# Hybrid network kernel: a third attention traced earlier, and a new order of projection chunks and output k-tiles

## The chip, the core and the metric

One core of a Trainium2 chip runs the whole kernel. The metric is the device time of one execution in microseconds; times given for a kernel are medians over its runs. Five engines work in order, each through its own queue of instructions: TensorE (PE in the profile, with its weight loads as PEld), VectorE (DVE), ScalarE (ACT), GpSimd (POOL) and SyncE (SP, which here issues the transfers from memory).

## The reference

The network has two blocks. The first is two "hybrid layers" on 256 tokens of width 1024; the second is one mixer (a state-space scan and an attention) and a mixture of 16 experts. The change is in the hybrid layer:

```python
def hybrid_layer(x, norm_w, w_in, w_out, conv_w, pe_cmp, w_cmp_k, w_cmp_v, pool_w, pool_scale):
    h = rmsnorm(x, norm_w)
    p = split_cols(h @ w_in)
    o_a = dsa_mixer(...)
    o_b = nsa_mixer(...)
    o_c = shortconv_mixer(p['c_b'], p['c_c'], p['c_x'], conv_w)
    o_d = pool_mixer(p['d_u'], pool_w, pool_scale)
    mixed = jnp.concatenate([jax.nn.silu(p['a_gate']) * o_a, jax.nn.silu(p['b_gate']) * o_b,
                             jax.nn.silu(p['c_gate']) * o_c, jax.nn.silu(p['d_gate']) * o_d], axis=-1)
    return x + mixed @ w_out
```

`dsa_mixer` is an attention over the keys that an index score picks; `nsa_mixer` is gated compressed attention plus two causal ones; `shortconv_mixer` is `b * conv(c * x)` with three taps; `pool_mixer` is a running mean over 2 to 16 tokens, less the token, times a small matrix. Each branch is 256 wide.

## The kernel before, in words

All arithmetic is in float32. A matrix product with full accuracy is made of three: each operand is split into a high and a low part, and `mm3` (L419, L420, L421) adds high by high, high by low and low by high. The weights are split on the chip piece by piece, the high part `whi` by ACT (L318), the low part `wlo` by DVE (L319).

The weights come as a stream of chunks of up to 2 MB in the order of the table `CHUNKS`, into a ring of four buffers; SP issues each transfer, and a buffer is given back as soon as its last piece is split. `run_pieces` takes the chunks piece by piece: it traces the split of the next piece at high priority, then runs the matmuls of the piece before, then that piece's closing work (`post_...`), and then grants the *side queue* a fixed credit (`SIDE_RATE`, 2.0 in layer 0 and 2.4 in layer 1). The side queue (`Side`) is first in, first out: generators that hold the small work of the branches, each step of which says what it costs in credit. From the order in which all this is traced, with its priorities, a scheduler writes the queue of each engine.

A hybrid layer (`layer`) is made of eleven chunks. Behind the first projections come four chunks in pairs of halves: the gates of the branches a and b, then `c_c` and `c_x`, `c_b` and `c_gate` for the convolution, then `d_u` and `d_gate` for the pooling (in the table `CHUNKS` and in the loop near the end of `layer`). Each half is a projection of 256 columns, 48 matmuls of 128x256, whose result is scaled (`gate_of`, L886, for gates) and whose `post_...` pushes the branch's work to the side queue:

- `post_gate(1)` pushes `b_branches`: the two causal attentions of branch b. Each has scores (L520 the mask, L533 the products), a softmax on DVE and ACT (L543, L545, L548, L549, L554), transposes of the probabilities (`prob_t`, L566, copied by ACT at L568) and the product with the values (`pv`, L575, into `obank`).
- `post_cc`, `post_cx`, `post_cb` and `post_cg` make the convolution: `cu`, then `cy` in six steps (L942, L944), the product with `cb` (L954), the gate's tanh (L891) and `sg` (L893), and the product of the two (L963).
- `post_du` makes the running sums on DVE up to `pl` (L990, L992), multiplies them by the small matrix on TensorE (L997), and copies the result to `yd` on ACT (L1000). `post_dg` multiplies `yd` by its gate.
- `post_dg`, the last of them, also pushes `a_branch`, the third attention: the same helpers with branch a's queries, keys `kaT` and its selection mask `selm`.

Each branch ends with `put_mixed`: ACT stores the high part in `mh` (L510), DVE the low part in `ml` (L511). These are eight k-tiles: a has 0 and 1, b 2 and 3, c 4 and 5, d 6 and 7.

Then come the two halves of the output projection, 512 columns each, in four pieces of two k-tiles, in the order of `MIX_ORDER`: 4, 5, 6, 7, 2, 3, 0, 1. Its matmuls are 128x512, `pj<-whi,mh` in the rows. Before the third piece of the first half the whole side queue is run (`side.finish`). `post_out` adds the halves to `X` (L1034), and `start_layer` transposes `X` for the next layer (L410).

The stages by time: layer 0 to about 155 us, layer 1 to about 296, the second mixer to about 435, the router to about 445, the experts to 690, the last norm to the end.

Of the kernel before, what the change touches and what calls it, by code (L numbers as in the profile page):

```python
# [42 lines left out]
for _n, _w in SPLITS:  # L43
# [1 line left out]
    _o += _w  # L45
CHUNKS = (("a_qi", "a_ki", "a_wi", "a_k", "a_v", "b_g"), ("a_q", "b_q"),
          ("b_ks", "b_kw", "b_vs", "b_vw", "b_kc", "b_vc"), ("a_gate", "b_gate"),
          ("c_c", "c_x"), ("c_b", "c_gate"), ("d_u", "d_gate"))
ORDER = tuple(4 * (p % 4) + p // 4 for p in range(N_EXP))
EXPERT_CHUNKS = [c for e in range(N_EXP - 1) for c in ((e, 0), (e, 1)) + (((e - 1, 2),) if e else ())]  # L50
EXPERT_CHUNKS += [(N_EXP - 2, 2), (N_EXP - 1, 0), (N_EXP - 1, 1), (N_EXP - 1, 2)]
MIX_ORDER = (4, 5, 6, 7, 2, 3, 0, 1)


def _ktiles(w):
# [191 lines left out]
class Net:  # L247
# [260 lines left out]
    def put_mixed(self, k, val, n=2):  # L508

        self.nc.scalar.activation(self.mh[:, k:k + n, :], val, AF.Copy)  # L510
        self.nc.vector.tensor_sub(self.ml[:, k:k + n, :], val, self.mh[:, k:k + n, :].bitcast(F32))  # L511

    def scores(self, t, qT, kT, mask, fb=None, f0=0):

# [119 lines left out]
    def layer(self, l):  # L634
        nc, wk, V = self.nc, self.wk, self.nc.vector
        X, side = self.X, self.side
# [3 lines left out]
        def tile2(name, tag="A", bufs=6):  # L640
            return wk.tile([P, 2, T], F32, name=name, tag=tag, bufs=bufs)
# [17 lines left out]
        def start1():  # L659
            if l == 0:  # L660
                self.start_layer(1, "nw0")
            self.mh = self.mx.tile([P, KT, T], F32R, name="mh")
            self.ml = self.mx.tile([P, KT, T], F32R, name="ml")

        def post0(pj):
            tk = S["tk"] = wk.tile([P, NT, 436], F32, name="tk", bufs=1)
            for t in range(NT):
                nc.scalar.activation(tk[:, t, :], pj[t][:, :436], AF.Copy, scale=S["rstd"][:, t:t + 1])
            side.push(prep0())
            side.push(index())  # L670
# [212 lines left out]
        def gate_of(ps):  # L883

            g = tile2("gate")
            V.scalar_tensor_tensor(g, ps, 0.5, rB(), op0=OP.mult, op1=OP.mult)  # L886
            return g

        def silu(g, tag="A", bufs=6):
            th = tile2("th")  # L890
            nc.scalar.activation(th, g, AF.Tanh)  # L891
            s = tile2("sg", tag, bufs)
            V.scalar_tensor_tensor(s, th, 1.0, g, op0=OP.add, op1=OP.mult)  # L893
            return s

        def post_gate(i):
            def post(ps):
                def f(g=gate_of(ps)):
                    S[f"sg{i}"] = silu(g, f"sgab{i}", 1)
                    yield 0.6  # L900
                side.push(f())
                if i == 1:
                    side.push(b_branches())
            return post

        def b_branches():
            qT, kbT, gs, tv = S["qT"], S["kbT"], S["gs"], S["tv"]
            O = None
            for br in range(2):
                pT = wk.tile([P, 2, 2, T + P], F32, name="probT", bufs=1)  # L910
                for t in range(NT):
                    sc = self.scores(t, qT[:, 2:4, :], kbT[:, br, :], self.caus[:, T - (t + 1) * P:])
                    g = gs[:, t, :].rearrange("p (j e b) -> p b e j", j=2, e=2)[:, 1 + br]
                    p = yield from self.softmax(t, sc, g)
                    self.prob_t(pT, t, p)
                    yield 0.1
                if O is None:
                    O = self.o_bank()
                    for j in range(2):
                        nc.tensor.matmul(O[:, j, :], self.vB[:, j, :], S["cpT"], start=False, stop=False)  # L920
                self.pv(O, tv[:, :, 128 + 64 * br:192 + 64 * br], pT, br == 1)
            m = tile2("mixv")
            V.tensor_mul(m, O, S["sg1"])
            yield 0.6
            self.put_mixed(2, m)
            yield 0.6
# [77 lines left out]
        def post_dg(ps):  # L1004
            def f(g=gate_of(ps)):
                s = silu(g)
                yield 0.6
                V.tensor_mul(s, s, S["yd"])
                yield 0.6
                self.put_mixed(6, s)  # L1010
                yield 0.6
            side.push(f())
            side.push(a_branch())

        def a_branch():
            pT = wk.tile([P, 2, 2, T + P], F32, name="probT", bufs=1)
            for t in range(NT):
                sc = self.scores(t, S["qT"][:, 0:2, :], S["kaT"], S["sel"][t][:, :(t + 1) * P])
                p = yield from self.softmax(t, sc)
                self.prob_t(pT, t, p)  # L1020
                yield 0.1
            O = self.o_bank()
            self.pv(O, S["tk"][:, :, 360:424], pT, True)
            m = tile2("mixv")
            V.tensor_mul(m, O, S["sg0"])
            yield 0.6
            self.put_mixed(0, m)
            yield 0.6
# [18 lines left out]
        yield from self.tok_pieces(w, None, 256, xh, xl, post2)  # L1047
        S["wc"], S["wcr"] = self.load()
        yield from self.col_pieces(w, r, 256, 1, xh, xl, post3)
        for a, b in ((post_gate(0), post_gate(1)), (post_cc, post_cx), (post_cb, post_cg), (post_du, post_dg)):  # L1050
            w, r = self.load()
            yield from self.col_pieces(w, None, 0, 2, xh, xl, a)
            yield from self.col_pieces(w, r, 256, 2, xh, xl, b)
        for h in range(2):
            w, r = self.load()
            yield from self.tok_pieces(w, r, HALF, Lazy(self, "mh"), Lazy(self, "ml"), post_out(h), order=MIX_ORDER,
                                       pre=(None, None, side.finish) if h == 0 else ())


    def row(self, i, t=None, n=D, eng=None):  # L1060
# [355 lines left out]
    def all_pieces(self):  # L1416
        tc, nc = self.tc, self.nc
        with ExitStack() as st:
            self.wk = w = st.enter_context(tc.tile_pool(name="wk", bufs=1, side="right"))
            self.kp = w.tile([P, 2, 528], F32, name="kp")  # L1420
            self.kB = w.tile([P, 2, 32], F32, name="kB")
            self.vB = w.tile([P, 2, P], F32, name="vB")
            self.cu = w.tile([P, 2, T + 2], F32, name="cu")
            self.du = w.tile([P, 2, T + 16], F32, name="du")
            for t in (self.kp, self.kB, self.vB):
                nc.gpsimd.memset(t, 0.0)
            nc.gpsimd.memset(self.cu[:, :, 0:2], 0.0)
            nc.gpsimd.memset(self.du[:, :, 0:16], 0.0)
            for l in range(DEPTH):
                self.phase = l  # L1430
                yield from self.layer(l)
                if self.stop == f"layer{l}":
                    yield FLUSH
                    self.dump()
                    return
            yield FLUSH
        with ExitStack() as st:
            self.wstack = st
            self.rw = st.enter_context(tc.tile_pool(name="rw2", bufs=1, side="right", reuse_waits="tile"))
            self.wk = w = st.enter_context(tc.tile_pool(name="wk2", bufs=1, side="right", reuse_waits="tile"))  # L1440
            self.mh = self.mx.tile([P, KT, T], F32R, name="mh")
            self.ml = self.mx.tile([P, KT, T], F32R, name="ml")
            self.ohf = w.tile([P, 16], BF16, name="ohfb")
            nc.vector.tensor_copy(self.ohf, self.c("ohf"))
            self.triTb = w.tile([P, T + P], BF16, name="triTb")
            nc.gpsimd.memset(self.triTb, 0.0)
            self.lb = self.mx.tile([P, 2, P], BF16, name="lb")
            nc.vector.tensor_add(self.lb[:, 0, :], self.c("causal")[:, P:], self.ident)
            nc.gpsimd.memset(self.lb[:, 1, :], 1.0)
            for c in (0, T):  # L1450
                nc.vector.tensor_scalar(self.triTb[:, c:c + P], self.lb[:, 0, :], -1.0, 1.0, op0=OP.mult, op1=OP.add)
            self.cw2 = w.tile([P, 8, 5], F32, name="cw2")
            nc.vector.tensor_scalar(self.cw2, self.c("convw2", 8, 5), 0.5, None, op0=OP.mult)
            self.xb = [w.tile([P, 2, T + 3], F32, name=f"xb{i}") for i in range(2)]
            self.nxb = 0
            for t in self.xb:
                nc.gpsimd.memset(t[:, :, 0:3], 0.0)
            self.phase = 2
            yield from self.second_mixer()
            yield FLUSH  # L1460
            if self.stop == "mix":
                self.dump()
# [553 lines left out]
```

## Time and profile before

| | |
|---|---|
| runs | 706.91 us median of 3 (706.5 to 707.29) |
| profiled execution | 710.95 us, span 709.1 us, mean granted clock 0.941 |
| TensorE busy | 636.0 us (90%) |
| DVE busy | 451.9 us (64%) |
| ACT busy | 307.5 us (43%) |
| POOL busy | 6.3 us (1%) |
| read from HBM | 161.57 MB, 229 GB/s over the span |

The times of all rows are of the one profiled execution, in us from the span's start. An instruction that waits shows as idle time of its engine, and a wait is put down to the instruction that released it ("PE bank L566 <- DVE prob L554": TensorE's instruction of line 566 waited for DVE's of line 554). The granted clock of TensorE is a share of full speed, 1.00 being 2.4 GHz.

### The profile page before, as it was taken

Reading aid. Unit: us, or ns where it says so; the run is one execution under the profiler, and the core shown is the slowest. Engines: PE = TensorE matmul, PEld = TensorE weight load, DVE = VectorE, ACT = ScalarE, POOL = GpSimd, SP = SyncE. Lnnn points to the kernel's source line nnn. Section 1 sums busy time; section 2 is a strip of 40 time slices with the busy share of each in tenths; the row PEclk is TensorE's granted clock in tenths of the full one; section 3 lists DMA queues with packets and bytes.
Section 4 is the critical chain, followed back from the end, with each engine's and each line's share of the span. In section 5 each row is a group of like instructions: output and inputs, shape, how many; then the busy total and the mean of one; then the engine's idle time right before and its main releaser. Section 6 shows DMA issues by size and latency. Waiting matters only on the chain. (4 is left out here: it accounts for less than half of the span.)

```text
span 709.1 us, 11794 instructions
## 1 busy us (share of the span) xinstructions
PE 636.0 (90%) x4466; PEld 448.3 (63%) x4466; DVE 451.9 (64%) x1064; ACT 307.5 (43%) x601; POOL 6.3 (1%) x28
## 2 busy tenths in 40 slices
PE   7999997999999989999999979968988897999762
PEld 4789885688898876898889767522532352263221
DVE  5898778477997694697768876725243433443426
ACT  5763644366635454543645433233232333233321
POOL 1000000000000000000000000000000000000001
PEclk9999998799999998999999988999997999899986
DMA  8956325015363042546303259699998899899811
GB/s 318 425 175 236 112 88 208 0 61 215 142 238 120 5 142 96 233 168 237 121 1 134 105 216 401 274 373 427 427 378 338 366 428 417 316 425 418 325 64 59
DMA packets 15920, 163.68 MB, mean 231 GB/s; under 512 B 1888, under 2 KB 2144, under 8 KB 6624
## 3 DMA queue, kind: packets, MB, share of 16 engines
q1 hardware_dynamic: 15552, 161.84, 57.3%
q8 instruction: 48, 0.79, 0.4%
q10 hardware_dynamic: 288, 0.79, 0.3%
q14 instruction: 32, 0.26, 0.1%
HBM read 161.57 MB, written 1.05 MB: 229 GB/s over the span
## 5 line engine op out<-in xcount | busy, mean ns | idle before, releaser
L318 ACT ACTIVATE whi<-wchunk 128x1024 fp32r<-128x1024 f32 (+2 forms) x103 | 107.4, 1043 | 97.2 <-PE pj L420 49.6
L319 DVE TENSOR_TENSOR wlo<-wchunk,whi 128x1024 fp32r<-128x1024 f32 (+2 forms) x103 | 123.2, 1197 | 26.7 <-ACT whi L318 26.4
L420 PE MATMUL pj<-xl,whi 128*128 128x256 f32 (+1 forms) x440 | 125.9, 286 | 0.0
L419 PE MATMUL pj<-xh,whi 128*128 128x256 f32 (+1 forms) x440 | 125.2, 285 | 0.0
L421 PE MATMUL pj<-xh,wlo 128*128 128x256 f32 (+1 forms) x440 | 125.1, 285 | 0.0
L420 PEld LDWEIGHTS pj<-xl,whi 128*128 128x128 f32 (+1 forms) x440 | 82.3, 187 | 3.3 <-issue 2.5
L419 PEld LDWEIGHTS pj<-xh,whi 128*128 128x128 f32 (+1 forms) x440 | 82.1, 187 | 1.8 <-issue 1.2
L421 PEld LDWEIGHTS pj<-xh,wlo 128*128 128x128 f32 (+1 forms) x440 | 82.3, 187 | 1.3 <-issue 0.9
L1691 PE MATMUL gu<-wchunk,xg 128*32 128x512 f32 x512 | 59.5, 605 | 0.6 <-DVE wq L1629 0.3
L419 PE MATMUL pj<-whi,mh 128*128 128x512 f32 x96 | 41.1, 428 | 2.1 <-ACT mh L510 2.1
L1731 DVE TENSOR_TENSOR tg<-tg,gu 64x256 f32<-64x256 f32 x32 | 13.2, 412 | 45.4 <-ACT tg L1730 45.4
L420 PE MATMUL pj<-wlo,xh 128*128 128x512 f32 (+2 forms) x112 | 40.4, 360 | 1.6 <-DVE wlo L319 1.6
L420 PE MATMUL pj<-wlo,mh 128*128 128x512 f32 x96 | 40.3, 420 | 0.0
L421 PE MATMUL pj<-whi,xl 128*128 128x512 f32 (+2 forms) x112 | 39.9, 356 | 0.0
L419 PE MATMUL pj<-whi,xh 128*128 128x512 f32 (+2 forms) x112 | 39.0, 354 | 0.9 <-ACT whi L318 0.9
L421 PE MATMUL pj<-whi,ml 128*128 128x512 f32 x96 | 39.4, 419 | 0.0
L1691 PEld LDWEIGHTS gu<-wchunk,xg 128*32 128x32 f32 x512 | 15.4, 111 | 32.3 <-issue 31.3
L1698 PE MATMUL dn<-wchunk,aT 128*64 128x512 f32 x112 | 30.7, 697 | 5.1 <-ACTq L1736 2.3
L1657 PE MATMUL acc<-y,oT 128*128 128x512 f32 (+1 forms) x80 | 26.9, 470 | 9.1 <-ACT y L1800 7.7
L1730 ACT ACTIVATE tg<-gu 64x256 f32<-64x256 f32 x32 | 12.2, 380 | 51.8 <-PE gu L1691 31.7
L545 ACT ACTIVATE prob<-bank,smst 128x128 f32<-128x128 f32 (+1 forms) x64 | 26.1, 418 | 17.0 <-DVE smst L543 17.0
L1691 PE MATMUL dn<-wchunk,aT 128*32 128x512 f32 x176 | 25.5, 705 | 7.9 <-ACT tg L1730 3.8
(404 smaller groups left out, 1064.6 us busy)
## 6 DMA issues: line engine op xcount, KB each, us to landing
wchunk<-wstream SPq DMA_DIRECT2D x67, 2048.0 KB, 11.5
wchunk<-wstream SPq DMA_DIRECT2D x12, 512.0 KB, 14.0
wchunk<-wstream SPq DMA_DIRECT2D x2, 1536.0 KB, 9.7
wchunk<-wstream SPq DMA_DIRECT2D x2, 1024.0 KB, 8.9
wchunk<-wstream SPq DMA_DIRECT2D x4, 436.0 KB, 5.7
wchunk<-wstream SPq DMA_DIRECT2D x1, 1744.0 KB, 6.8
wchunk<-xt SPq DMA_DIRECT2D x4, 256.0 KB, 5.4
X<-x SPq DMA_DIRECT2D x4, 256.0 KB, 6.0
```

What stands on the lines that cost most here:

```text
L318: nc.scalar.activation(hi, w, AF.Copy)
L319: nc.vector.tensor_sub(lo, w, hi.bitcast(F32))
L419: mm(out, ah, bh, start=start, stop=False)
L420: mm(out, ah, bl, start=False, stop=False)
L421: mm(out, al, bh, start=False, stop=stop)
L545: nc.scalar.activation(p[:, e, j, :N], S[e][:, j, :], AF.Exp, bias=nm[:, e, j:j + 1], accum_out=sm[:, e, j:j + 1])
L1657: self.nc.tensor.matmul(self.acc[t][h], oT[r, t * P:(t + 1) * P], y[1 + i], start=False, stop=last and i == 1, **at)
L1691: self.nc.tensor.matmul(out[r:r + 32, :], lhs(k), w(k)[:, HALF * i:HALF * i + HALF], start=(k < 2), stop=(k >= n - 2), tile_position=(0, r))
L1698: self.nc.tensor.matmul(out[64 * i:64 * i + 64, :], lhs(k), w(k)[:, HALF * i:HALF * i + HALF], start=(k == 0), stop=(k == n - 1), tile_pos ...
L1730: nc.scalar.activation(tg[0:64, 0, s], b[64:128, s], AF.Copy)
L1731: V.tensor_add(tg[0:64, 0, s], tg[0:64, 0, s], b[0:64, s])
```

## The change

The third attention is pushed to the side queue right behind the other two. The pooling's chunk goes ahead of the convolution's two, in the weight stream and in the loop. The order of k-tiles in the output projection becomes 2, 3, 0, 1, 6, 7, 4, 5. Before each of the four pieces of the first output half the side queue is run, in steps of credit 0.5, only until the first of the piece's own k-tiles has been stored; the pair is stored by one call of `put_mixed`.

```diff
 CHUNKS = (("a_qi", "a_ki", "a_wi", "a_k", "a_v", "b_g"), ("a_q", "b_q"),
           ("b_ks", "b_kw", "b_vs", "b_vw", "b_kc", "b_vc"), ("a_gate", "b_gate"),
-          ("c_c", "c_x"), ("c_b", "c_gate"), ("d_u", "d_gate"))
+          ("d_u", "d_gate"), ("c_c", "c_x"), ("c_b", "c_gate"))
...
-MIX_ORDER = (4, 5, 6, 7, 2, 3, 0, 1)
+MIX_ORDER = (2, 3, 0, 1, 6, 7, 4, 5)
...
         self.nc.scalar.activation(self.mh[:, k:k + n, :], val, AF.Copy)
         self.nc.vector.tensor_sub(self.ml[:, k:k + n, :], val, self.mh[:, k:k + n, :].bitcast(F32))
+        self.mixed.add(k)
+
+    def need(self, k):
+
+        def f():
+            while k not in self.mixed:
+                self.side.run(0.5)
+        return f
...
             self.ml = self.mx.tile([P, KT, T], F32R, name="ml")
+            self.mixed = set()
...
                 if i == 1:
                     side.push(b_branches())
+                    side.push(a_branch())
...
                 self.put_mixed(6, s)
                 yield 0.6
             side.push(f())
-            side.push(a_branch())
...
-        for a, b in ((post_gate(0), post_gate(1)), (post_cc, post_cx), (post_cb, post_cg), (post_du, post_dg)):
+        for a, b in ((post_gate(0), post_gate(1)), (post_du, post_dg), (post_cc, post_cx), (post_cb, post_cg)):
             w, r = self.load()
...
-                                       pre=(None, None, side.finish) if h == 0 else ())
+                                       pre=[self.need(k) for k in MIX_ORDER[::2]] if h == 0 else ())
```

What this does to the queues is shown at three places of layer 0. Lines of the changed kernel are a few further down (L520 is L528 there, L533 is L541, L575 is L583, L942 to L963 are L952 to L973).

TensorE before, at the start of the output projection, between the matmuls of its first piece and those of its second. `pl` are the pooling's sums, `selm` is the third attention's mask, `prob` are its probabilities:

```order
L580 MATMUL obank<-zero 128x512
L997 MATMUL bank<-pl,cst 128x256 x2
L520 LDWEIGHTS negid
L520 MATMUL bank<-selm,negid 128x256
L520 LDWEIGHTS negid
L520 MATMUL bank<-selm,negid 128x256
L533 MATMUL bank<-kaT,qT 128x128 x4
L566 MATMUL bank<-cstm,prob 128x128
L520 LDWEIGHTS negid
L520 MATMUL bank<-selm,negid 128x512
L566 MATMUL bank<-cstm,prob 128x128
```

After the change the same scores stand in the projections, beside the second attention's products with the values:

```order
L420 MATMUL pj<-xl,whi 128x256
L421 MATMUL pj<-xh,wlo 128x256
L528 LDWEIGHTS negid
L528 MATMUL bank<-selm,negid 128x256
L528 LDWEIGHTS negid
L528 MATMUL bank<-selm,negid 128x256
L541 MATMUL bank<-kaT,qT 128x128 x3
L583 MATMUL obank<-probT,tv 64x128 x4
L583 MATMUL obank<-probT,tv 64x256 x4
L541 MATMUL bank<-kaT,qT 128x128
L419 MATMUL pj<-xh,whi 128x256
```

The third attention has moved from the output projection into the convolution's projections; the pooling matmul L997 (L1007 now) follows it there.

DVE before, in the same stretch: the third attention's scalings (L548 to L554), its product with the gate (L1025) and the storing of its `ml` between two splits, and then the first half's addition to `X`:

```order
L548 TENSOR_SCALAR smst<-smst 128x4
L549 RECIPROCAL smst<-smst 128x4
L554 TENSOR_SCALAR prob<-prob,smst 128x256 x4
L319 TENSOR_TENSOR wlo<-wchunk_975,whi 128x1024
L1025 TENSOR_TENSOR mixv<-obank,sg 128x512
L511 TENSOR_TENSOR ml<-mixv,mh 128x512
L319 TENSOR_TENSOR wlo<-wchunk_975,whi 128x1024
L1034 TENSOR_TENSOR X<-X,pj 128x512 x2
```

After the change, DVE at the same place. `sg_1477` is the pooling's product (k-tiles 6 and 7), `sg_1541` the convolution's (4 and 5), `wchunk0_794` and `wchunk1_974` are the two output halves:

```order
L952 TENSOR_SCALAR cy_1513<-cu_148,cst_81 128x256 x2
L954 SCALAR_TENSOR_TENSOR cy_1513<-cu_148,cst_81,cy_1513 128x256 x2
L511 TENSOR_TENSOR ml_213<-sg_1477,mh_212 128x512
L954 SCALAR_TENSOR_TENSOR cy_1513<-cu_148,cst_81,cy_1513 128x256
L319 TENSOR_TENSOR wlo_1563<-wchunk0_794,whi_1562 128x1024
L954 SCALAR_TENSOR_TENSOR cy_1513<-cu_148,cst_81,cy_1513 128x256
L902 SCALAR_TENSOR_TENSOR sg_1541<-th_1539,gate_1508 128x512
L964 TENSOR_TENSOR cb_1425<-cy_1513,cb_1425 128x512
L319 TENSOR_TENSOR wlo_1581<-wchunk1_974,whi_1580 128x1024
L973 TENSOR_TENSOR sg_1541<-sg_1541,cb_1425 128x512
L319 TENSOR_TENSOR wlo_1624<-wchunk1_974,whi_1623 128x1024
L511 TENSOR_TENSOR ml_213<-sg_1541,mh_212 128x512
```

Here the convolution's steps are the last work before the output projection's fourth piece, and two splits of the second output half (`wlo_1581`, `wlo_1624`) stand among them.

TensorE after the change, where the fourth piece of the first half (`whi_1562`, k-tiles 4 and 5) begins. `whi_1580` and `whi_1623` are pieces of the second half:

```order
L421 MATMUL pj_1522<-whi_1543,ml_213 128x512
L419 MATMUL pj_1627<-whi_1580,mh_212 128x512
L420 MATMUL pj_1627<-wlo_1581,mh_212 128x512
L421 MATMUL pj_1627<-whi_1580,ml_213 128x512
L419 MATMUL pj_1627<-whi_1580,mh_212 128x512
L420 MATMUL pj_1627<-wlo_1581,mh_212 128x512
L421 MATMUL pj_1627<-whi_1580,ml_213 128x512
L419 MATMUL pj_1627<-whi_1623,mh_212 128x512
L419 MATMUL pj_1521<-whi_1562,mh_212 128x512
L420 MATMUL pj_1521<-wlo_1563,mh_212 128x512
```

The scheduler has put matmuls of the second half, which need only k-tiles 2, 3 and 0, ahead of the first half's last piece. On SP and POOL the order is as before; in layer 1 the moves are of the same kind.

## Rows read from the trace of the kernel before

**Rows 1.** The page's slices: TensorE's busy tenths, and its granted clock.

```profile
PE   7999997999999989999999979968988897999762
...
PEclk9999998799999998999999988999997999899986
```

**Rows 2.** Waits of TensorE: us in all, times, longest; 95:152, 235:300, 56:115.

```profile
PE bank L566 <- DVE prob L554: 2.8, 1, 2.8
PE bank L997 <- DVE pl L992: 2.7, 1, 2.7
...
PE bank L566 <- DVE prob L554: 3.8, 2, 3.3
PE bank L997 <- DVE pl L992: 0.3, 1, 0.3
...
PE bank L566 <- DVE prob L554: 0.5, 1, 0.5
```

**Rows 3.** Windows: us, PE (x), PEld, DVE, ACT, POOL, granted clock, DMA, GB/s.

```profile
73.00:90.00 17.00, 16.50 (x133) 13.78 (x133) 12.09 (x33) 9.58 (x31) 0.00 (x0) 1.00 0.27 95
100.00:115.00 15.00, 15.00 (x115) 14.31 (x115) 14.79 (x25) 6.98 (x8) 0.00 (x0) 1.00 0.37 141
118.20:121.80 3.60, 3.57 (x14) 2.32 (x14) 0.46 (x1) 1.36 (x3) 0.00 (x0) 0.50 0.81 273
124.60:134.40 9.80, 9.80 (x25) 6.14 (x26) 3.96 (x12) 2.53 (x9) 0.00 (x0) 0.50 0.00 0
267.90:274.60 6.70, 6.70 (x18) 4.26 (x18) 2.49 (x8) 2.53 (x9) 0.00 (x0) 0.51 0.31 132
```

**Rows 4.** Timeline of TensorE: start, duration (us), instruction; projections, output projection.

```profile
81.14 0.28 PE L420 MATMUL pj<-xl,whi 128*128 128x256 f32 x1
81.26 0.28 PE L421 MATMUL pj<-xh,wlo 128*128 128x256 f32 x1
...
134.83 0.39 PE L419 MATMUL pj<-whi,mh 128*128 128x512 f32 x1
135.06 0.39 PE L420 MATMUL pj<-wlo,mh 128*128 128x512 f32 x1
```

**Rows 5.** Timeline of DVE in layer 1's projections.

```profile
244.91 0.35 DVE L942 TENSOR_SCALAR cy<-cu,cst 128x256 f32<-128x256 f32 x1
...
247.11 0.48 DVE L944 SCALAR_TENSOR_TENSOR cy<-cu,cst,cy 128x256 f32<-128x256 f32 x1
247.50 0.68 DVE L886 SCALAR_TENSOR_TENSOR gate<-pj,rB 128x512 f32<-128x512 f32 x1
248.10 0.68 DVE L954 TENSOR_TENSOR cb<-cy,cb 128x512 f32<-128x512 f32 x1
248.70 1.22 DVE L319 TENSOR_TENSOR wlo<-wchunk,whi 128x1024 fp32r<-128x1024 f32 x1
249.84 0.68 DVE L893 SCALAR_TENSOR_TENSOR sg<-th,gate 128x512 f32<-128x512 f32 x1
```

**Rows 6.** Timeline of ACT at the end of layer 1; in brackets its wait.

```profile
262.87 0.84 ACT L1000 ACTIVATE yd<-bank,cst 128x256 f32<-128x256 f32 x2 [0.61 <-PE bank L997]
...
264.21 0.63 ACT L891 ACTIVATE th<-gate 128x512 f32<-128x512 f32 x1 [0.51 <-DVE gate L886]
```

**Rows 7.** Two other waits of TensorE (40:56, 415:424), each with a window behind it.

```profile
PE bank L839 <- ACT whi L318: 1.3, 1, 1.3
...
52.00:54.00 2.00, 0.73 (x7) 0.55 (x6) 2.00 (x14) 1.06 (x1) 0.00 (x0) 1.00 0.66 238
...
PE bank L345 <- DVE diag L344: 1.5, 1, 1.5
...
421.20:428.00 6.80, 4.86 (x12) 3.79 (x12) 2.19 (x4) 0.94 (x2) 0.00 (x0) 0.50 0.89 377
```

**Rows 8.** Windows before the experts and in them.

```profile
445.00:450.00 5.00, 5.00 (x29) 4.72 (x28) 4.11 (x16) 1.95 (x3) 0.00 (x0) 1.00 0.19 46
460.00:690.00 230.00, 194.80 (x1330) 81.59 (x1330) 90.39 (x176) 72.84 (x139) 0.00 (x0) 0.93 0.88 363
```

More of the change, by code (lines that the diff above doesn't have):

```diff
@@ L1442, in all_pieces @@
             self.ml = self.mx.tile([P, KT, T], F32R, name="ml")
+            self.mixed = set()
             self.ohf = w.tile([P, 16], BF16, name="ohfb")
```

## The prediction

> **What bounds the kernel now.** I began with the page's slices, numbered from 0, of 17.7 us each. TensorE is busy in nine tenths or more of nearly all of them up to slice 22; it dips at slice 6 and at 14, and the granted clock dips with it or right behind, at slices 6, 7 and 15 [rows 1]. These are the ends of the two hybrid layers, where the output projection starts. The waits of TensorE name the two causes there: the pooling matmul L997 waits for DVE's `pl`, and the third attention's transposes L566 wait for DVE's `prob`: 2.7 and 2.8 us in layer 0, 0.3 and 3.8 us in layer 1 [rows 2]. The windows give what follows: the granted clock drops from 1.00 to 0.50 (2.4 to 1.2 GHz) and stays there after the waiting is over, in layer 0 up to 134.4, in layer 1 from 267.9 to 274.6 [rows 3]. Before these ends TensorE is the bound, 15.00 of 15.00 us from 100 to 115. DVE has room from 73 to 90, 12.09 of 17 us, and none from 100 to 115, 14.79 of 15 [rows 3]. At the full clock TensorE starts a matmul of 256 columns 0.12 us after the one before it, one of 512 columns 0.23 us after it [rows 4].
>
> So the two layer ends lose, against a TensorE that never waits: layer 0, 2.7 + 2.8 = 5.5 us of waiting, and 3.57 + 9.80 = 13.4 us of work at half clock, which would be 6.7 us at full clock; layer 1, 0.3 + 3.8 = 4.1 us and half of 6.70, 3.4 us. Together **19.7 us**. That is the most that the change can take back here.
>
> **The change, part by part.** Nothing is computed more or less. SP's queue keeps its order and sizes: the chunk that goes ahead is as large as the two it passes. POOL's order is untouched too.
>
> *The third attention moves.* Its scores now stand in the convolution's projections, a matmul or two behind the second attention's transposes. Everything it issues moves along: masks, scores, transposes and values on TensorE, 12 exponentials and copies on ACT, reductions and scalings on DVE. Its TensorE time stays the same, and the stretch it leaves loses the waits of 2.8 and 3.8 us. The price is what it waits for in the new place. The nearest row is the second attention's transposes, the same code in the same surroundings: 0.5 us in layer 0 [rows 2]. That is the lower end. The upper end is the old wait of 2.8 us. In layer 0 DVE's queue holds, between the third attention's 256-wide scores and their scaling, two 512-wide multiplies and a split more than the second's, 0.6 + 0.6 + 1.1 us by their starts [rows 5]; TensorE has 28 matmuls of 256 columns to cover it, 3.4 us, as the second attention has 27 and still waits 0.5. I take **1.5 us a layer**, 0.8 at each of the two transposes, nearer to the second attention's row than to the old wait.
>
> *The pooling goes ahead.* In layer 0 its matmul L997 now follows the third attention's value product by 57 matmuls of 256 and 5 of 512 columns: 57 x 0.12 + 5 x 0.23 = 8.0 us. DVE's work between the two is five 512-wide operations, two splits and eight small ones: 5 x 0.6 + 2 x 1.14 + 8 x 0.35 = 8.1 us [rows 5]. I take no wait; the bounds are 0 and the old 2.7 us. Layer 1 is alike.
>
> *The convolution comes last.* Now k-tile 4 must be ready when the last piece of the first output half starts, and DVE works through a queue to get there. After L997, ACT makes `yd` and the tanh, 0.84 + 0.63 us [rows 6], and only then DVE's queue goes on. In layer 0 it holds, up to the product that k-tile 4 is copied from, seven 512-wide operations at 0.61, two 256-wide scalings at 0.35, four steps of the convolution at 0.4 and two splits at 1.14 us, 8.9 us [rows 5]; ACT's copy, as wide as the tanh, adds 0.63. So the tile is there 1.5 + 8.9 + 0.6 = 11.0 us after L997. TensorE has 38 matmuls of 512 columns and a clear until then, 39 x 0.23 = 9.0 us. **It waits 2.0 us**, mostly at the first matmul that needs `wlo_1581`, which stands on DVE ahead of that product. Layer 1: eight 512-wide, two scalings, four steps and four splits are 11.7 us, so the tile comes after 13.8 us; TensorE has 49 starts at 0.23 and 12 at 0.12, 12.7 us. **It waits 1.1 us.** The bounds are 0, if the sum on DVE is 2 us too long, and 3.8 us, the longest wait of the old ends [rows 2].
>
> *The drain per tile.* A piece of the first output half now runs the side queue only until its own two k-tiles are stored, where before its third piece ran all of it. The wait moves to the fourth piece, and is the one priced above. The second output half had no drain and has none.
>
> *The clock.* Which of the new waits costs the clock? After a wait of 1.3 us near 53 the granted clock stayed at 1.00; after one of 1.5 us near 420 it fell, and stood at 0.50 for 6.8 us [rows 7]; after 2.7 us and more it fell too [rows 2, 3]. So 2.0 us in layer 0 lies among those that lost it, 1.1 us in layer 1 among those that kept it. I take one fall, in layer 0, at the price of a fall in layer 1 now: 6.7 us of work at half clock [rows 3], 3.4 us. The bounds are none and two.
>
> *What comes after.* The queues of the second mixer are reordered by a few places, with the same instructions; its end has a wait of 1.5 us now [rows 7]. I take 0, with 1.5 us to either side. The shift then carries to the end: from 445 to 450 the DMA engines are busy only 0.19 of the time, against 0.88 from 460 to 690 [rows 8]. The four buffers of the ring are full then, so the long run of transfers starts when compute frees a buffer, and moves with it.
>
> *Sum.* 19.7 - 2 x 1.5 - 2.0 - 1.1 - 3.4 = **10.2 us saved**. The profiled execution took 710.95 us around a span of 709.1, 4.0 us over the median of the runs; I set the saving against the median: 706.9 - 10.2 = **696.7 us**, 1.4% less.
>
> **The rivals.**
>
> *The clock holds in both layers.* For it: layer 1's wait is short, and 2.0 us rests on a DVE sum that may be 1 us long. Against it: the fall after 1.5 us [rows 7]. It saves 19.7 - 3.0 - 3.1 = 13.6 us: 693.3.
>
> *Both ends fall, and the convolution is later than counted.* For it: DVE is full, 14.79 of 15 us [rows 3], in the stretch that now takes the third attention's work, so anything late is passed down the same queue. Two falls cost 6.8, and another 1.2 us of waiting per layer 2.4: 19.7 - 3.0 - 3.1 - 6.8 - 2.4 = 4.4 us saved: 702.5.
>
> *Slower: the clock falls in the stretch that is now full.* The third attention cuts the projections into short runs with a wait between them. If each of its four waits, two a layer, brought a fall of 3.4 us, that is 13.6 us more: 696.7 + 13.6 = 710.3. From three falls on, all but nothing of the saving is left. Against it: from 73 to 90 the second attention does just this, with TensorE at 16.50 of 17 us and a granted clock of 1.00 [rows 3]. The Trainium skill ("TensorE: Matmul & The Clock Gate", A second HAM failure mode: psum-queue depth-cycling) says that a kernel that often idles briefly between groups of matmuls makes the clock swing between its two levels and loses throughput so. By that rule this change would be of this kind; the trace does not agree for the second attention, whose clock held.
>
> *No change: the saving does not reach the end.* If the experts' transfers ran at their limit from a fixed time on, the end would stay at 706.9. The idle DMA engines at 445 to 450 speak against it [rows 8]. That the move is not made at all is excluded by the order of the instructions.
>
> **How the numbers follow.** Forecast 696.7 us with a chance of 0.44; the clock holds in both, 0.22; both fall and late, 0.20; no change, 0.06; slower, 0.08. About 0.2%, 1.4 us, is what a measurement of this kernel can tell from no change. Faster gathers the first three, 0.86; same 0.06; slower 0.08. The range takes in the two neighbours, with the 1.5 us of the later stages partly added: 690.5 to 704.0; about 0.19 lie outside.
>
> **What would show it.** In the changed profile TensorE's waits at the end of layer 0 should no longer hold L997 or L566 with 2.7 and 2.8 us, but one wait of about 2.0 us on a split or on `mh`, in layer 1 about 1.1 us; L566 on `prob` in two waits of 0.8 us a layer; a clock of 0.50 for about 7 us in layer 0 and none at the end of layer 1. The stretch of nearly idle DMA engines before the experts should come about 10 us earlier. The forecast is wrong if DVE's queue makes the convolution later than 4 us, if the clock falls in the projections, or if the experts start earlier but end at the same time.

## The result and the profile after

The changed kernel took 697.3 us (median of 4 runs, 696.26 to 698.28) beside 707.1 us for the kernel before: a ratio of 0.986, 95% interval 0.984 to 0.989, so 9.8 us less. The forecast was 696.7 us. Its profiled execution took 696.77 us around a span of 695.0.

The page of the changed kernel, the line of its engines, and the slices that answer to [rows 1]:

```profile
PE 626.3 (90%) x4466; PEld 443.4 (64%) x4466; DVE 451.6 (65%) x1064; ACT 306.8 (44%) x601; POOL 6.3 (1%) x28
...
PE   7999999899899999999999989878979897999762
...
PEclk9999999999999999999989998989998998899986
```

TensorE does the same 4466 matmuls in 9.7 us less busy time, and the clock's dips at slices 6, 7 and 15 are gone. The waits of TensorE at the two layer ends (layer 0 from 100 to 155, layer 1 from 235 to 295; us in all, times, longest) answer to [rows 2]:

```profile
PE pj L420 <- DVE wlo L319: 1.9, 1, 1.9
PE bank L574 <- ACT whi L318: 0.4, 1, 0.4
PE bank L1007 <- DVE pl L1002: 0.3, 1, 0.3
...
PE bank L1007 <- DVE pl L1002: 0.6, 1, 0.6
PE pj L420 <- DVE wlo L319: 0.6, 1, 0.6
PE bank L574 <- DVE prob L562: 0.3, 1, 0.3
```

In place of 9.6 us of waiting there are 4.1 us: 2.5 for splits behind the convolution's steps, 0.9 for the pooling's `pl`, 0.7 for the third attention. The 9.6 us hold 0.45 us that the change did not touch. Of the 3.8 us that [rows 2] gives for layer 1, the third attention's wait is the longest, 3.3; the other is the second attention's (TensorE's timeline before):

```profile
238.14 0.63 PE L566 MATMUL bank<-cstm,prob 128*128 128x128 f32 x4 [0.45 <-DVE prob L554]
```

The same wait stands at 229.34 after the change, ahead of the window. Like for like, 9.1 us became 4.1. The windows over both ends (columns as in [rows 3]; the granted clock is the third number from the right) show it at full speed:

```profile
110.00:150.00 40.00, 37.83 (x213) 31.04 (x212) 31.38 (x52) 20.85 (x36) 0.00 (x0) 1.00 0.33 119
235.00:295.00 60.00, 58.05 (x375) 48.58 (x373) 46.77 (x94) 30.24 (x54) 0.00 (x0) 1.00 0.38 150
```

How far each layer has come is read from DVE's addition of its second output half to `X` (timeline; start, duration):

```profile
145.92 1.39 DVE L1043 TENSOR_TENSOR X<-X,pj 128x512 f32<-128x512 f32 x2
...
282.51 1.28 DVE L1043 TENSOR_TENSOR X<-X,pj 128x512 f32<-128x512 f32 x2
```

In the first profiled execution of the kernel before it stands at 154.53 and 295.75:

```profile
154.53 1.39 DVE L1034 TENSOR_TENSOR X<-X,pj 128x512 f32<-128x512 f32 x2
...
295.75 1.28 DVE L1034 TENSOR_TENSOR X<-X,pj 128x512 f32<-128x512 f32 x2
```

So 8.6 us are won by the end of layer 0 and 13.2 by the end of layer 1, and the span as a whole is 14.1 shorter. That is more than the 9.8 us of the medians, because that execution of before took 710.95 us, 4 us over its median; the first experiment looks at that.

### The profile page after: what moved, and what is told of

It reads as the page before. It is cut to its first block, busy times and chain, and to the rows that moved or that the text cites. A ratio compares the mean times of both kernels' runs of the same rounds, so it can differ in the third digit from the quotient of the medians.

```text
span 695.0 us, 11796 instructions
## 1 busy us (share of the span) xinstructions
PE 626.3 (90%) x4466; PEld 443.4 (64%) x4466; DVE 451.6 (65%) x1064; ACT 306.8 (44%) x601; POOL 6.3 (1%) x28
## 5 line engine op out<-in xcount | busy, mean ns | idle before, releaser
L419 PE MATMUL pj<-xh,whi 128*128 128x256 f32 (+1 forms) x440 | 126.8, 289 | 0.0
L1741 DVE TENSOR_TENSOR tg<-tg,gu 64x256 f32<-64x256 f32 x32 | 13.2, 412 | 46.5 <-ACT tg L1740 46.4
L419 PE MATMUL pj<-whi,mh 128*128 128x512 f32 x96 | 38.5, 404 | 2.6 <-ACT mh L510 2.1
L420 PE MATMUL pj<-wlo,mh 128*128 128x512 f32 x96 | 38.1, 398 | 2.5 <-DVE wlo L319 2.5
L421 PE MATMUL pj<-whi,ml 128*128 128x512 f32 x96 | 37.5, 400 | 0.0
L1708 PE MATMUL dn<-wchunk,aT 128*64 128x512 f32 x112 | 28.9, 663 | 4.8 <-PEq L1779 2.8
L1701 PE MATMUL mbs<-wchunk,xg 128*32 128x512 f32 x288 | 32.2, 592 | 0.0
```

The lines of the kernel that those rows point to most:

```text
L419: mm(out, ah, bh, start=start, stop=False)
L420: mm(out, ah, bl, start=False, stop=False)
L421: mm(out, al, bh, start=False, stop=stop)
L1701: self.nc.tensor.matmul(out[r:r + 32, :], lhs(k), w(k)[:, HALF * i:HALF * i + HALF], start=(k < 2), stop=(k >= n - 2), tile_position=(0, r))
L1708: self.nc.tensor.matmul(out[64 * i:64 * i + 64, :], lhs(k), w(k)[:, HALF * i:HALF * i + HALF], start=(k == 0), stop=(k == n - 1), tile_pos ...
L1741: V.tensor_add(tg[0:64, 0, s], tg[0:64, 0, s], b[0:64, s])
```

## The experiments

**The kernel before, profiled again** (no edit).

> The kernel before, unchanged, profiled a second time, since its first profiled execution took 710.95 us, 4.0 us more than the median of its runs. Theory A (the extra 4 us of that execution are chance falls of the clock outside the layer ends): about 707 us; the layer ends show the same waits of 2.7 and 2.8 us in layer 0 and 3.3 us in layer 1 and the same stretches at 0.50, 13.4 and 6.7 us of work; the clock differs elsewhere, by some 4 to 8 us of work at half clock. Rival B (a typical execution holds the clock longer at the layer ends than the profiled one): about 707 us, with 8 us less work at 0.50 at the layer ends and the rest alike.

It took 708.81 us, span 707.0. The waits are the same to 0.1 us. The addition of the second half to `X` in both layers, and the windows over both layer ends, with the first execution's window over layer 0's end ahead of them:

```profile
153.12 1.39 DVE L1034 TENSOR_TENSOR X<-X,pj 128x512 f32<-128x512 f32 x2
...
294.41 1.28 DVE L1034 TENSOR_TENSOR X<-X,pj 128x512 f32<-128x512 f32 x2
```

```profile
110.00:150.00 40.00, 34.51 (x157) 25.14 (x156) 24.45 (x46) 17.56 (x40) 0.00 (x0) 0.79 0.21 83
...
110.00:150.00 40.00, 34.50 (x161) 25.39 (x161) 25.06 (x47) 18.03 (x40) 0.00 (x0) 0.83 0.23 86
235.00:295.00 60.00, 55.91 (x342) 45.49 (x340) 42.38 (x76) 28.73 (x56) 0.00 (x0) 0.94 0.28 104
```

Neither theory is right as it stood: 1.3 us of the difference lies at layer 0's end, where the clock was low for a shorter time (a mean of 0.83 against 0.79 in the first execution), and the rest, 0.8 of 2.1 us, behind the layers. The waits repeat; how long the clock stays low after them does not. Against this execution the change wins 11.9 us by the end of layer 1 and 12.0 in the span. TensorE's busy time up to that end falls from 277.28 to 268.98 us, by 8.3 for the same matmuls, and its idle time by the other 3.6.

**Dummy work in the waits of the kernel before.**

```diff
+                if l == 0:
+                    wb = self.bank()
+                    for _ in range(5):
+                        nc.tensor.matmul(wb[:, :T], self.c(f"poolw{l}", 2, P)[:, 0, :], d2[:, 0, 16:], start=True, stop=True)
                 py = self.bank().rearrange("p (a t) -> p a t", a=2)
...
+        if warm is not None:
+            wb = self.bank()
+            for _ in range(2):
+                nc.tensor.matmul(wb[:4, :], st[:, 0:4], warm, start=True, stop=True)
         yield 0.7 + 0.6 * t
```

(the second in `softmax`, behind the row maxima, with branch a's queries as `warm` for the third attention's first half.)

> The kernel before with matmuls whose results nobody reads placed into TensorE's waits: five of 128x256 that need only the pooling's sums ahead of L997 in layer 0, and in each layer two of 4x512 that need the third attention's row maxima, ahead of its first transposes. The DVE work that is waited for is as before, so the waiting time isn't won, only the clock. Theory A (about half of what the layer ends lose is the clock, and the clock falls because TensorE stands idle): granted clock 1.00 through both layer ends, 6.7 + 3.4 = 10 us less, some 1 us back for what the added matmuls overshoot: about 698 us. Rival B (it falls for another reason, or the added matmuls don't count): 0.50 as before, 707 us or up to 2 us more.

It took 699.05 us (696.92 to 704.97, 7 runs), ratio 0.988, 0.985 to 0.992. TensorE's timeline at layer 0's end: the added matmuls are L1001 and L550. The pooling's matmul waits 0.40 us now instead of 2.70. The third attention's first transposes (122.07), which waited 2.79, show no wait any more; those of its second half (127.85) wait 0.18.

```profile
113.46 2.40 PE L1001 MATMUL bank<-d,cst 128*128 128x256 f32 x10
...
117.19 1.13 PE L1005 MATMUL bank<-pl,cst 128*128 128x256 f32 x4 [0.40 <-DVE pl L996]
...
120.25 1.88 PE L550 MATMUL bank<-qT,smst 128*4 128x512 f32 x4
122.07 0.32 PE L570 MATMUL bank<-cstm,prob 128*128 128x128 f32 x1
...
127.85 0.41 PE L570 MATMUL bank<-cstm,prob 128*128 128x128 f32 x2 [0.18 <-DVE prob L558]
```

```profile
285.40 1.28 DVE L1042 TENSOR_TENSOR X<-X,pj 128x512 f32<-128x512 f32 x2
```

The clock was 1.00 through both ends, and layer 1 ended at 285.40, 9.0 us before the second execution of the kernel before, although the third attention, the pooling and the convolution come in the order in which they came. That is theory A. The added matmuls fill 5.7 us, and TensorE's idle time by the end of layer 1 falls by the same 5.7, from 17.1 to 11.4 us; so the 9.0 us are busy time of the kernel's own matmuls.

It is not the clock alone. The scheduler answered the added matmuls with small moves in layer 0: on DVE a split and a store of `ml` went behind the third attention's first scalings, so that `pl` was ready 0.8 us earlier, and on TensorE a few matmuls changed places. With the 8.3 us of busy time that the change itself saves, 8 to 9 of its 11.9 us are the clock, and 3 to 4 the shorter waiting.

**The third attention left last.**

```diff
-MIX_ORDER = (2, 3, 0, 1, 6, 7, 4, 5)
+MIX_ORDER = (2, 3, 6, 7, 4, 5, 0, 1)
...
                     side.push(b_branches())
-                    side.push(a_branch())
...
                 self.put_mixed(4, s)
                 yield 0.6
             side.push(f())
+            side.push(a_branch())
```

> The change without its first part: chunks in the new order (pooling ahead of the convolution), drains per tile, but the third attention pushed last, behind the convolution's gate; k-tile order 2, 3, 6, 7, 4, 5, 0, 1. Theory A (moving the third attention away from the end is what pays): its transposes wait again for DVE at the layer ends, 2 to 4 us a layer, the clock falls in at least one of them, 700 to 704 us. Rival B (the chunk order and the drain per tile do it, since the pooling's sums and the convolution are then ready early): 696 to 698 us.

701.62 us (4 runs), ratio 0.991, 0.988 to 0.995: the middle of theory A's range, but not as expected. The waits at the layer ends are many and short, and the clock held:

```profile
PE obank L583 <- ACT probT L576: 1.1, 1, 1.1
PE bank L574 <- DVE prob L562: 1.0, 1, 1.0
PE obank L588 <- DVE mixv L1034: 0.8, 1, 0.8
...
PE bank L574 <- DVE prob L562: 1.7, 1, 1.7
```

Even without the early third attention 7 us of the 9.8 are won: no wait is longer than 1.7 us, and none of them cost the clock in this execution.

**The pooling left last** (the third attention early, the old chunk order).

```diff
-          ("d_u", "d_gate"), ("c_c", "c_x"), ("c_b", "c_gate"))
+          ("c_c", "c_x"), ("c_b", "c_gate"), ("d_u", "d_gate"))
...
-MIX_ORDER = (2, 3, 0, 1, 6, 7, 4, 5)
+MIX_ORDER = (2, 3, 0, 1, 4, 5, 6, 7)
```

> The change without its second part: the third attention pushed right behind the first two and drains per tile, but chunks in the old order, the pooling last; k-tile order 2, 3, 0, 1, 4, 5, 6, 7. Theory A (the early third attention is enough; the pooling then has the matmuls of six k-tiles to hide behind): TensorE waits 1 to 2.5 us a layer for the pooling's tile, clock 1.00, 697 to 700 us. Rival B (the pooling's long chain over DVE, TensorE, ACT and DVE must not be last): waits of 3 us and more a layer with a clock fall in each, 702 us or more.

693.82 us (4 runs), ratio 0.981, 0.976 to 0.985: better than either theory gave, so it was put beside the changed kernel on one chip.

> The changed kernel once more, to stand beside the next one on the same chip. Both theories: 697 to 698 us; clock 1.00 through both layer ends.

> The version with the third attention early and the pooling still last, once more, beside the changed kernel. Theory A (putting the convolution last costs what TensorE waits there more, 2.5 + 0.9 us of waits on splits and on the pooling's sums against 1.5 us on the stored tile): 2 to 3.5 us less than the changed kernel, 694 to 695.5 us. Rival B (the two orders are alike, and the first comparison was chance): within 1 us of it, 697 us.

The changed kernel took 698.02 us (6 runs, 696.35 to 699.65; ratio 0.986), this version 694.93 (6 runs, 693.97 to 695.25; ratio 0.981, 0.978 to 0.984): theory A, 3.1 us. Its waits at the layer ends, and the end of layer 1, which the changed kernel beside it reached at 283.84:

```profile
PE pj L419 <- ACT mh L510: 1.2, 1, 1.2
PE bank L574 <- DVE prob L562: 0.4, 1, 0.4
...
PE pj L419 <- ACT mh L510: 0.2, 1, 0.2
```

```profile
281.81 1.28 DVE L1043 TENSOR_TENSOR X<-X,pj 128x512 f32<-128x512 f32 x2
```

The tile of the pooling is waited for 1.2 + 0.2 us, where the convolution's order costs 2.5 + 0.9; that is 2.0 of the 3.1 us. The rest comes behind the layers and is not explained. Each of the six runs was shorter than each of the changed kernel's six. So the new chunk order, with the k-tile order that goes with it, costs time, and this version beats both kernels.

**A longer wait in the changed kernel.**

```diff
+                if l == 0:
+                    for _ in range(3):
+                        V.tensor_scalar(S["y"], S["y"], 1.0, None, op0=OP.mult)
                 V.tensor_mul(cb, S["y"], cb)
```

> The changed kernel with three more 128x512 operations on DVE in layer 0 only (a multiplication by one), ahead of the convolution's product, so that the output projection's last piece waits longer. Theory A (waiting costs the clock once TensorE stands idle for more of a stretch than the 1.9 us of the changed kernel): 1.5 us more waiting, the clock falls to 0.50 at layer 0's end for some 7 us of work, 3.4 us: about 702 us. Rival B (the clock held there because the work around it is dense, however long the wait): clock 1.00, 1.5 us more: about 699 us.

This did not decide between the two. One such operation takes DVE 0.33 us, not 0.5, and the scheduler put more matmuls of the second half ahead of the last piece: TensorE waited 1.96 and 0.55 us, not 1.9 and 1.5 more, and the clock held. Layer 0 ended at 147.20, 1.3 us later than in the first profiled execution of the changed kernel (145.92). The second, profiled beside this one, ended layer 0 at 147.19 as well, but for another reason: its clock was low near 17 us, ahead of everything that the change moves (window of that execution; the first has 1.00 there, and so has this run):

```profile
15.00:20.00 5.00, 4.37 (x16) 4.11 (x17) 3.26 (x10) 1.25 (x3) 0.00 (x0) 0.66 1.02 413
```

The time was 700.63 us (4 runs), some 2.6 over the changed kernel; by the profiles, half of that came from behind the layers. So the same with ten operations, which leaves the queues as they are with three but for one matmul:

> The changed kernel with ten more 128x512 operations on DVE in layer 0 instead of three (0.33 us from one to the next in the run with three, where TensorE's waits there were 1.96 and 0.55 us and the clock held). Theory A (a wait of more than the 1.9 us costs the clock): the second wait grows by 7 x 0.33 = 2.3 us to about 2.9 us, the clock stands at 0.50 for several us of work behind it, 2.3 + 1.7 to 3.4 us more than the run with three: 704 to 706 us. Rival B (the clock holds at this place however long the wait): clock 1.00, 2.3 us more: about 703 us.

706.05 us (10 runs, 700.49 to 708.32), ratio 0.995, 0.992 to 0.999. The wait in question (TensorE's timeline), and a window ahead of it and one behind:

```profile
140.00 0.80 PE L419 MATMUL pj<-whi,mh 128*128 128x512 f32 x1 [3.80 <-ACT mh L510]
```

```profile
133.30:136.20 2.90, 2.89 (x11) 1.91 (x11) 2.80 (x6) 0.00 (x0) 0.00 (x0) 1.00 0.96 393
140.00:145.70 5.70, 5.70 (x15) 4.35 (x16) 1.53 (x3) 0.12 (x1) 0.00 (x0) 0.51 0.01 3
```

Theory A: in the same place, with the same matmuls around it, 3.80 us of waiting cost the clock (0.51 from 140.0 to 145.7), where the 1.96 and 0.55 of the run with three did not, nor the 1.95 that comes first in this one. Layer 0 ended 7.2 us later than with three (154.42 against 147.20). Of these, 1.6 were there before the output projection's waits, with a low clock near 17 us again; 3.2 are more waiting, and the 2.4 that are left are the clock. The Trainium skill ("TensorE: Matmul & The Clock Gate", HAM oscillation — how this bites in real kernels) describes this for waits on data between bursts of matmuls: the next burst starts throttled. The run with 3.80 us agrees, at 0.51 behind the wait. It is one profiled execution, and its time, 708.25 us, is near the top of the ten runs; whether the fall is in each of them is not shown.

**The drain alone.** With the old order of chunks, k-tiles and third attention, the drain per tile gives the same queues on every engine, so no run was made of that. In the new order it was taken back:

```diff
-                                       pre=[self.need(k) for k in MIX_ORDER[::2]] if h == 0 else ())
+                                       pre=(side.finish,) if h == 0 else ())
```

> The changed kernel with the whole side queue run ahead of the first output piece instead of a drain per tile. On TensorE and DVE only a few places differ: at layer 0's end the last piece comes some matmuls earlier among the second half's, and one split goes behind the convolution's steps; ACT, SP and POOL are the same. Theory A (the drain per tile adds nothing of its own, the order of chunks and of the third attention does it): 697 to 698.5 us. Rival B (the drain keeps the last piece from blocking TensorE): 2 us and more slower, 699.5 us or above.

698.20 us (6 runs, 696.59 to 700.18), ratio 0.986: theory A. Layer 0's wait of 1.9 us for a split is one of 2.0 us for `mh` instead.

**A fall of the clock without a wait.** In `router_weights`, in the second mixer, for both of its loops:

```diff
+            if k % 4 == 3:
+                self.clear(wb)
```

> The changed kernel with four 128x512 matmuls on zeros, whose results nobody reads, put into the second mixer's run of 34 matmuls of 20 columns (one after every four of the two groups of eight). Theory A (the clock fell near 353 because that run, though it counts as busy and has no wait, is little work for the array): the clock holds near 353, 3.4 us less, 0.9 us of it back for the added matmuls: 2.5 us less than the changed kernel, about 695 us. Rival B (it fell for another reason): it falls as before, 0.9 us more, about 698 us.

The clock was 1.00 there (351.8 to 362.0), but the time stayed, 698.38 us (6 runs) beside 698.02. With the added matmuls the scheduler also put the attention's products with its values (16 matmuls) into the run of 20 columns, so the matmuls on zeros are not the only difference. In the profiled execution the clock had fallen at layer 0's end, 1.4 us of work behind the wait of 1.9 us that cost nothing in two other executions:

```profile
133.00:136.40 3.40, 3.40 (x10) 2.60 (x9) 0.89 (x2) 0.00 (x0) 0.00 (x0) 0.50 0.37 153
351.80:362.00 10.20, 10.20 (x91) 9.20 (x89) 6.47 (x12) 3.26 (x5) 0.00 (x0) 1.00 0.00 0
```

> The version with the third attention early and the pooling last (693.82 and 694.93 us in two comparisons), with the four matmuls on zeros in the second mixer's run of 20-column matmuls. In the changed kernel they held the clock near 353, and yet the time stayed, with falls in other places. Theory A (the fall there is real work lost, and what came instead was chance): clock 1.00 from 345 to 362, about 2.5 us less than that version, 692 us. Rival B (a fall that is kept off in one place comes in another soon after): the same time, 694 to 695 us, with more falls behind the second mixer.

694.23 us (5 runs, 692.32 to 695.26), ratio 0.980, 0.978 to 0.983, the clock at 1.00 from 345 to 362: rival B's time. The two profiles show where the saving went. At the matmuls of L345 near 406, in the second mixer's output projection, this execution was 2.3 us ahead of the version without the added matmuls (405.70 against 408.01), as theory A has it. Behind them the clock fell from 409.0 to 412.5, where it held in the other, and the experts began only 0.8 us earlier (439.18 against 439.97). Whether keeping the first fall off brought the second is open: among the eight profiled executions of the changed kernel and its variants that lost the clock near 350 to 360, four lost it again at this place and four did not.

## Why the prediction was right, and where it was off

**The bound and the place** were right: against the second execution of before, 11.9 of the 12.0 us are there at the end of layer 1.

**The third attention's waits** were put at 1.5 us a layer and measured 0.4 and 0.3, as little as the row that was called nearest, the 0.5 of [rows 2]. That row is the first attention's, at 84.72, ahead of the second's scores at 85.93; and the 0.4 is put down to ACT's split, not to `prob`. **The pooling** was put at 0 and measured 0.3 and 0.6. **The convolution last** was put at 2.0 and 1.1 and measured 1.9 and 0.6. The queue that was counted is the one that shows: in layer 0 TensorE waits for the split that stands on DVE between the two products of the convolution (timelines of DVE and TensorE):

```profile
129.78 0.68 DVE L964 TENSOR_TENSOR cb<-cy,cb 128x512 f32<-128x512 f32 x1
130.38 1.22 DVE L319 TENSOR_TENSOR wlo<-wchunk,whi 128x1024 fp32r<-128x1024 f32 x1
131.51 0.68 DVE L973 TENSOR_TENSOR sg<-sg,cb 128x512 f32<-128x512 f32 x1
```

```profile
131.65 0.50 PE L420 MATMUL pj<-wlo,mh 128*128 128x512 f32 x1 [1.89 <-DVE wlo L319]
```

**The drain** cost and gave nothing, as counted.

**The clock is the term that was mis-sized.** The prediction said: "I take one fall, in layer 0", 3.4 us. In the first two profiled executions of the changed kernel there was none at the layer ends; in a third, with the same work in layer 0, there was one (0.50 from 133.0 to 136.4), and layer 0 ended 1.5 us later than in the first. Two readings behind the term were off.

The first is that of [rows 7]: the fall near 420 was put down to one wait of 1.5 us. But a second wait, of 2.1 us for `mh`, follows 0.7 us later, and the clock fell at 421.2, when that wait had begun (timeline of before, then windows):

```profile
420.32 0.71 PE L345 MATMUL bank<-diag,ones 128*128 128x128 f32 x4 [1.48 <-DVE diag L344]
...
423.14 0.79 PE L419 MATMUL pj<-whi,mh 128*128 128x512 f32 x1 [2.11 <-ACT mh L510]
```

```profile
420.30:421.00 0.70, 0.68 (x4) 0.52 (x4) 0.16 (x1) 0.00 (x0) 0.00 (x0) 1.00 1.11 234
421.60:422.00 0.40, 0.00 (x0) 0.00 (x0) 0.40 (x2) 0.00 (x0) 0.00 (x0) 0.50 0.22 82
```

This pair of waits stands at the second mixer's end in every profile. In the three of the kernel before and its version with dummy work the clock fell there each time, but in the other two only behind the second wait (at 423.1 and 414.0, for waits that ended at 421.83 and 412.93). In the ten of the changed kernel and its variants, where the pair is 0.8 and 2.1 us, it fell in six and held in four. The changed kernel's 1.9 us at layer 0's end held in two executions and fell in one. So waits of this length were a chance, and the prediction counted the one in layer 0 as lost. Which executions lose the clock, and why, stays open.

The second is the price: work at 0.50 was taken as twice as long as at 1.00. The starts of 512-column matmuls at 0.50 lie 0.43 us apart, not twice the 0.23 of [rows 4] (timeline of before):

```profile
130.82 0.63 PE L421 MATMUL pj<-whi,ml 128*128 128x512 f32 x1
131.24 0.63 PE L419 MATMUL pj<-whi,mh 128*128 128x512 f32 x1
```

By that ratio the 20.1 us of slow work of the layer ends can give back some 9.1 us, not 10.1 (an estimate); TensorE's busy time up to the end of layer 1 fell by 9.0, as the two windows below show. By profile the rival "the clock holds in both layers" (13.6 us saved) is what happened: 13.2 us by the end of layer 1, against the execution from which its terms were read.

**Why the total was right all the same.** Up to the end of layer 1 TensorE's idle time fell by 4.3 us (295.75 - 277.95 to 282.51 - 268.98) and its busy time by 9.0, together 13.2:

```profile
0.00:295.75 295.75, 277.95 (x2035) 233.66 (x2036) 221.51 (x547) 158.52 (x321) 2.49 (x14) 0.96 0.43 161
```

```profile
0.00:282.51 282.51, 268.98 (x2036) 228.26 (x2037) 220.60 (x547) 157.94 (x321) 2.49 (x14) 1.00 0.44 166
```

The sum had 3.5 us less waiting and 6.7 less for the clock, 10.2. For the profiled execution of before it would give 710.95 - 10.2 = 700.8 us; the changed kernel's profiled execution took 696.77. What hid this error is that the saving was set against a median 4 us lower than the execution that showed the 19.7 us. That the two cancelled is luck. The 13.2 us are no fixed amount either: against the second execution of before they are 11.9, and between the executions that lie nearest to their medians (708.81 and 698.16 us) 10.6 (294.41 to 283.84), of which the last step, 1.3, is the low clock near 17 us.

**The slower rival** did not come: 0.4 us was the longest wait that the third attention's move brought, and the clock held through the projections. **What comes after** was 0 only in sum. Against the second execution of before, the lead was 11.9 us at the end of layer 1, 9.2 at the first matmuls on the experts' weights (441.62 against 450.84) and 12.0 at the end; behind the layers the clock falls at other places in each execution.

## What to carry to other kernels

Here some 9 us of waiting on TensorE came with as much again in the clock behind it. To tell the two apart, fill the wait with matmuls that nobody reads, made to depend on an earlier step of the same chain: what this wins is about the clock's share, here 8 to 9 of 11.9 us. Then compare the queues, since the scheduler may move other work when instructions are added.

Test the parts of a reordering one by one: here the early third attention with the old chunk order was 3 us better than the whole change. And before a term is read from one profiled execution, see how far that execution lies from the median, and set two profiles side by side from a common point, since a low clock ahead of the change shifts all that follows (1.3 us here).

## What the hardware showed that was not expected

The clock fell without a wait. In the second mixer of the changed kernel TensorE is busy all the time from 349.9 on, with 34 matmuls of only 20 columns each, and the clock goes from 1.00 to 0.50 among them, near 352.8 (timeline, then windows):

```profile
349.91 1.86 PE L1493 MATMUL bank<-wg,ones 128*128 128x20 f32 x16
351.61 2.48 PE L1495 MATMUL bank<-cst,cstm 128*128 128x20 f32 x16
```

```profile
349.90:352.50 2.60, 2.60 (x26) 2.60 (x25) 1.13 (x1) 1.09 (x2) 0.00 (x0) 1.00 0.00 0
353.00:359.00 6.00, 6.00 (x31) 4.64 (x31) 2.72 (x8) 0.60 (x1) 0.00 (x0) 0.50 0.00 0
```

With four matmuls of 512 columns and the attention's products among them it held, in both runs that had them; which of the two did it is not shown. And a wait of the same length, 1.9 us in the same place, cost the clock in one execution and not in two others, so such a term is a chance, not a fixed price.
